# The last token block of a down projection in two column pieces, and part of each block's results through ScalarE and GpSimd

## The chip, the cores and the metric

The kernel runs on one core of one Trainium2 chip. The metric is the device time of one execution in microseconds (us), as the median of several runs. In this text PE is TensorE (PEld its weight load), DVE VectorE, ACT ScalarE, POOL GpSimd and SP the engine that issues most of the DMAs. L1197 is line 1197 of the kernel before; lines of the changed kernel are called new lines.

## The reference

One layer of a hybrid encoder for two request groups, 256 prompt rows and 128 sample rows, 384 rows of 2048 channels in all, in fp32: a mixer (pooling branch, state-space branch, gates, output projection) and an MLP, each between two RMS norms. The part that matters here is the end of the MLP:

```python
def rmsnorm(x, g):
    xf = x.astype(jnp.float32)
    y = xf * lax.rsqrt(jnp.mean(xf * xf, axis=-1, keepdims=True) + EPS)
    return (y * g.astype(jnp.float32)).astype(x.dtype)
...
    x = x + rmsnorm(m, p['g_mix_post'])
    hdn = jnp.square(jax.nn.relu(rmsnorm(x, p['g_mlp_pre']) @ p['w_up'])) @ p['w_down']
    x = x + rmsnorm(hdn, p['g_mlp_post'])
```

`w_up` is 2048 x 8192 and `w_down` 8192 x 2048. The last norm needs the sum of squares over all 2048 columns of a row before any element of that row can be finished.

## The kernel before

All matrix products keep fp32's precision by splitting each operand into a high part and a rest, both of type fp32r (a shortened fp32), and adding three matmuls: high x high, high x rest, rest x high. A weight unit of 128 x 1024 values is fetched by `wfetch` (L59, on SP's queue) and split by `wsplit` (L64): ACT copies it to fp32r (L68), DVE subtracts (L69).

The MLP runs in eight rounds, `c8`. A round makes eight slices of the hidden layer (line 1164 on; products in `proj`, relu and square on DVE and ACT) and then multiplies them by `w_down` in four column tiles `nb` of 512 columns. For this `moving` (L110) is called with three PSUM tiles `o[b]`, one for each block of 128 token rows. The activations are the stationary operand, loaded afresh for every matmul, and the weights are the moving one, 512 columns wide. Inside `moving`, `mm` (L114) issues the three matmuls of one depth of 128 rows (L118, L119, L120). A down tile has four weight units of two such depths each, so a block takes 4 x 2 x 3 = 24 matmuls.

In all tiles but the last, a unit is used for all three blocks and then dropped. In the last tile of the last round (`c8` = 7, `nb` = 3) `tail` is 4: all four units are kept, and the loop at L138 runs all 24 matmuls of block 0, then of block 1, then of block 2, calling `done(b)` after each, so that the closing work of one block runs under the matmuls of the next. The fourth unit has its own buffers `eh` and `el` (L133 to L136), since the pool has three.

`done` (L1177) closes a block of a down tile:

- DVE adds the PSUM tile to the accumulator `hacc` (L1182).
- In the last round ACT squares the result, with the row sums going to one column of `st3` for each tile (L1186).
- In tiles 0 to 2 DVE multiplies by the norm's gain `gpo` in place (L1188). In tile 3 DVE writes the product to its own tile `z3` (L1193).
- In tile 3 `postnorm` (L943) follows, on 128 x 1 operands: DVE sums the first three partial sums (L945 to L947, which can run early), ACT takes a root with the fourth (L948), DVE makes the fourth's own sum (L949), a reciprocal (L950) and a correcting step (L951, L953). The result is `y`, one factor for each row.
- For each of the four column tiles DVE computes `z * y + x1` (L1197, 512 columns; `x1` is the residual held in SBUF) and SP stores 256 KB (L1200).

A framework orders the work: each engine runs its instructions in the order in which it was given them (a scheduler may let ready work pass; `behind` ties an instruction to follow another), and waits on semaphores are set where one engine reads what another wrote, or writes what another still reads. SP issues its stores in order, each behind its own wait. POOL has had its last instruction, the load of `gpo` (L1156), long before; ACT issues no DMA in this kernel.

Of the kernel before, what the change touches and what calls it, by code (L numbers as in the profile page):

```python
# [14 lines left out]
P = 128  # L15
# [4 lines left out]
DM = 2048  # L20
# [13 lines left out]
def build(ctx, tc, io):  # L34
# [21 lines left out]
    def behind(ins):  # L56
        return nullcontext() if ins is None else tc.issue_after(ins.ins)
# [22 lines left out]
    last = [None]  # L80
# [26 lines left out]
            half(o, q, take(src, f"{name}_{q}"), rhs)  # L107
        return o

    def moving(o, units, lhs, tail, done, pool=None, own=0, hook=None):  # L110
        nk = 2 * len(units)
        n = len(units)

        def mm(b, wh, wl, k, k2):  # L114
            t = slice(b * P, b * P + P)
            c = slice(k2 * 512, k2 * 512 + 512)
            mh, ml = lhs[k][0][:, t], lhs[k][1][:, t]
            te.matmul(o[b], mh, wh[:, c], start=k == 0, stop=False)  # L118
            te.matmul(o[b], mh, wl[:, c], start=False, stop=False)  # L119
            last[0] = te.matmul(o[b], ml, wh[:, c], start=False, stop=k == nk - 1)  # L120

        for kp in range(n - tail):
            wh, wl = take(*units[kp])
            with behind(last[0] if chain[0] else None):
                for k2 in range(2):
                    for b in range(3):
                        mm(b, wh, wl, kp * 2 + k2, k2)
            if hook and kp in hook:
                hook[kp]()
        w = [wload(*units[kp]) for kp in range(n - tail, n - own)]  # L130
        for kp in range(n - own, n):
            f, name = wfetch(*units[kp])
            h = pool.tile([P, 1024], F32R, name=f"eh_{name}")  # L133
            l = pool.tile([P, 1024], F32R, name=f"el_{name}")
            s.activation(h, f, AF.Copy)
            v.tensor_tensor(l, f, h.bitcast(F32), ALU.subtract)  # L136
            w.append((h, l))
        for b in range(3):  # L138
            for i, (wh, wl) in enumerate(w):
                for k2 in range(2):  # L140
                    mm(b, wh, wl, (n - tail + i) * 2 + k2, k2)
            done(b)

    def three(name):
        return [sstile(f"{name}_{b}") for b in range(3)]
# [167 lines left out]
    with tc.tile_pool(name="phc", bufs=1, reuse_waits="tile") as pc, tc.tile_pool(name="phc2", bufs=2, reuse_waits="tile") as pc2:  # L313
# [75 lines left out]
        def gate_a(nb):  # L389
            o = three(f"pj_ga{nb}")  # L390
            sg = pc2.tile([P, 3, 512], F32, tag="sg", name=f"sg{nb}", bufs=1)

            def done(b):
                s.activation(sg[:, b], o[b], AF.Sigmoid, scale=yx[:, b : b + 1])

            moving(o, [(io["w_ga"][nb, kp], f"ga{nb}_{kp}") for kp in range(8)], xg, 0, done)
            return sg

        def pool_out(nb, sg):
            o = three(f"pj_pp{nb}")  # L400

            def done(b):
# [92 lines left out]
    def gate_b(nb, pool, tag, hook=None):  # L495
        o = three(f"pj_gb{nb}")
        n = NB * 256 if tag == "hs" else 1536
        t = pool.tile([P, n], F32, tag=tag, name=f"gbt{nb}")[:, :1536].rearrange("p (b n) -> p b n", b=3)

        def done(b):  # L500
# [400 lines left out]
    with ExitStack() as phe:  # L901
        pe1 = phe.enter_context(tc.tile_pool(name="phe", bufs=1, reuse_waits="tile"))
        pe2 = phe.enter_context(tc.tile_pool(name="phe2", bufs=3, reuse_waits="tile"))
        pe4 = phe.enter_context(tc.tile_pool(name="phe4", bufs=1, reuse_waits="tile"))
        ab = []

        def aload():
            for i in (len(ab), len(ab) + 1):
                a = pe2.tile([P, T], F32, tag="ar", name=f"ar{i}")
                sy.dma_start(a, a_scr[i])  # L910
                h = pe1.tile([P, T], F32R, name=f"abh{i}")
                l = pe1.tile([P, T], F32R, name=f"abl{i}")
                s.activation(h, a, AF.Copy)
                v.tensor_tensor(l, a, h.bitcast(F32), ALU.subtract)
                ab.append((h, l))

        for nb in (2, 3):
            gate_b(nb, pe4, "gbt", {kp: aload for kp in range(8)})
        chain[0] = False
        main.close()  # L920
        mp = mpool.enter_context(tc.tile_pool(name="mp", bufs=1, side="right", reuse_waits="tile"))
        for nb in range(4):
            ma = mp.tile([P, 3, 512], F32, tag="mar", name=f"mar{nb}", bufs=1)
            gb = pe4.tile([P, 1536], F32, tag="gbt", name=f"gbr{nb}").rearrange("p (b n) -> p b n", b=3)
            sy.dma_start(ma, ma_scr[nb])
            sy.dma_start(gb, gb_scr[nb])
            o = three(f"pj_sp{nb}")

            def done(b):
# [8 lines left out]
    x1 = res.tile([P, 3, DM], F32, name="x1")  # L938
# [1 line left out]

    root = [None]

    def postnorm(pool, st, b, name, doubled=False):  # L943
        pre, ms, rt, y = (pool.tile([P, 1], F32, tag=f"n{i}", name=f"n{i}_{name}{b}", bufs=3) for i in range(4))
        v.tensor_tensor(pre, st[:, b, 0:1], st[:, b, 1:2], ALU.add)  # L945
        v.tensor_tensor(pre, pre, st[:, b, 2:3], ALU.add)
        v.tensor_scalar(pre, pre, 1.0 / DM, EPS, ALU.mult, ALU.add)  # L947
        root[0] = s.activation(rt, st[:, b, 3:4], AF.Sqrt, bias=pre, scale=1.0 / DM)  # L948
        v.tensor_scalar(ms, st[:, b, 3:4], 1.0 / DM, pre, ALU.mult, ALU.add)  # L949
        v.reciprocal(y, rt)  # L950
# [11 lines left out]
    with tc.tile_pool(name="phf", bufs=1, side="right", reuse_waits="tile") as pf, tc.tile_pool(  # L962
# [19 lines left out]
        for nb in range(4):  # L982
# [5 lines left out]
            def done(b):  # L988
# [162 lines left out]
    with tc.tile_pool(name="phg", bufs=1, reuse_waits="tile") as pg, tc.tile_pool(  # L1151
# [7 lines left out]
        pg.tile([P, 112], F32, name="pad_e")  # L1159
        NC = 8  # L1160
        for c8 in range(NC):
            hh = []
# [11 lines left out]
            for nb in range(4):  # L1174
                o = [sstile(f"wd{c8}_{nb}_{b}") for b in range(3)]

                def done(b):  # L1177
                    dst = hacc[:, b, blk(nb)]
                    if c8 == 0:
                        s.copy(dst, o[b])  # L1180
                        return
                    v.tensor_tensor(dst, o[b], dst, ALU.add)  # L1182
                    if c8 < NC - 1:
                        return
                    q = pg2.tile([P, 512], F32, tag="q3", name=f"q3_{nb}_{b}")
                    s.activation(q, dst, AF.Square, accum_out=st3[:, b, nb : nb + 1])  # L1186
                    if nb < 3:
                        v.tensor_tensor(dst, dst, gpo[:, blk(nb)], ALU.mult)  # L1188
# [3 lines left out]
                    z3 = pg.tile([P, 512], F32, name=f"z3_{b}")  # L1192
                    v.tensor_tensor(z3, dst, gpo[:, blk(nb)], ALU.mult)  # L1193
                    y = postnorm(pg2, st3, b, "n3", doubled=True)
                    for i in range(4):
                        z = z3 if i == 3 else hacc[:, b, blk(i)]
                        v.scalar_tensor_tensor(  # L1197
                            out=z, in0=z, scalar=y, in1=x1[:, b, blk(i)], op0=ALU.mult, op1=ALU.add
                        )
                        sy.dma_start(io["y"][b][:, blk(i)], z)  # L1200

                moving(
                    o,
# [128 lines left out]
```

## Time and profile before

| | |
|---|---|
| median of 3 runs | 2812.53 us (2811.7 to 2814.31) |
| the profiled execution, its own time | 2813.31 us |
| its span, from the first to the last instruction | 2811.5 us |
| mean granted TensorE clock | 0.999 |
| HBM read, written | 407.11 MB, 41.72 MB |
| all DMA, mean | 161 GB/s |
| matmuls of the down projection, L118 | 296.3 us busy in x762, mean 389 ns |
| PSUM adds of the down projection, L1182 | 57.3 us busy in x84, mean 691 ns |
| stores of the last block, L1200 | 12 of 256 KB in all three blocks, 2.3 us from issue to landing |

A row of the profile names the line, the engine, the operation, the tile written and the tiles read, the shape and the count. A matmul's busy time includes the time to run through the array, so neighbours overlap: matmuls of 389 ns each start 0.227 us apart. What one costs in a row of many is the distance between two starts. In a timeline row the first number is the start in us from the beginning of the span and the second the duration; what stands in brackets is the engine's idle time before it and who ended it. The profile's spans on POOL are rough.

### The profile page before, as it was taken

To read this page: it belongs to the slowest core of one execution; us is meant where nothing else is said; L and a number is where in the kernel's file an instruction comes from. 1 tells how busy PE (TensorE), PEld (TensorE's weight loads), DVE (VectorE), ACT (ScalarE), POOL (GpSimd) and SP (SyncE) were. 2 spreads that over 40 slices of the span, in tenths; PEclk is the share of its full clock that TensorE was granted. 3 is DMA by queue.
4 is the path that set the end of the run, shared out by engine and by line. 5 is a ranking of instruction groups with operands and counts; after the bars stand their busy time and mean duration, and the time that the engine had idled before them with its cause. 6 is when DMAs were issued, how large, how long until landed. Compare 5 with 4: busy or idle time off the path is not lost.

```text
span 2811.5 us, 39083 instructions
## 1 busy us (share of the span) xinstructions
PE 2795.5 (99%) x15663; PEld 2545.3 (91%) x15663; DVE 1487.7 (53%) x1979; ACT 1167.9 (42%) x1830; POOL 119.5 (4%) x143
## 2 busy tenths in 40 slices
PE   9999999999999999999999999999999999999998
PEld 8998889999999999988888888989899998989897
DVE  6575335677777778756333336434444444444446
ACT  5443225456565646544322235433233332323233
POOL 0000000001110111010000000000000000000000
PEclk9999999999999999999999999999999999999999
DMA  7434445555565556557544543433333343333333
GB/s 268 132 125 150 139 139 199 180 187 207 198 225 191 201 198 223 195 185 232 177 145 162 180 144 115 140 128 128 128 128 128 128 128 128 128 129 128 131 127 122
DMA packets 140934, 451.39 MB, mean 161 GB/s; under 512 B 17808, under 2 KB 39632, under 8 KB 135760
## 3 DMA queue, kind: packets, MB, share of 16 engines
q1 hardware_dynamic: 132624, 412.97, 44.6%
q0 software_dynamic: 8128, 35.93, 3.3%
q8 instruction: 123, 2.02, 0.3%
q14 instruction: 59, 0.48, 0.1%
HBM read 407.11 MB, written 41.72 MB: 160 GB/s over the span
## 4 chain that ended last, share of the span: by engine, by line
PE 97%; ACT 1%; DVE 1%; DMA 0%; issue 0%; SPq 0%; DVEq 0%; ACTq 0%
PE pj_up L77 6%; PE pj_up L78 6%; PE pj_up L76 6%; PE wd L119 6%; PE wd L120 6%; PE wd L118 6%; PE pj_x L76 4%; PE pj_x L77 4%; PE pj_x L78 4%; PE pj_z L77 3%; PE pj_z L78 3%; PE pj_z L76 3%; PE pj_sp L119 3%; PE pj_sp L120 3%; PE pj_sp L118 3%; PE pj_ga L118 2%
## 5 line engine op out<-in xcount | busy, mean ns | idle before, releaser
L76 PE MATMUL pj_up<-x1h,wh_up 128*128 128x384 f32 x1024 | 342.6, 335 | 0.5 <-ACT x1h L1058 0.5
L78 PE MATMUL pj_up<-x1h,wl_up 128*128 128x384 f32 x1024 | 342.3, 334 | 0.7 <-DVE wl_up L69 0.7
L77 PE MATMUL pj_up<-x1l,wh_up 128*128 128x384 f32 x1024 | 342.3, 334 | 0.6 <-DVE x1l L1063 0.6
L120 PE MATMUL wd<-wh_wd,hl 128*128 128x512 f32 x762 | 296.6, 389 | 0.0
L119 PE MATMUL wd<-wl_wd,hh 128*128 128x512 f32 x762 | 296.6, 389 | 0.0
L118 PE MATMUL wd<-wh_wd,hh 128*128 128x512 f32 x762 | 296.3, 389 | 0.0
L69 DVE TENSOR_TENSOR wl_wd<-w_wd,wh_wd 128x1024 fp32r<-128x1024 f32 x127 | 155.6, 1226 | 261.9 <-ACT wh_wd L68 261.9
L68 ACT ACTIVATE wh_wd<-w_wd 128x1024 fp32r<-128x1024 f32 x127 | 134.8, 1061 | 350.8 <-PE wd L120 284.2
L68 ACT ACTIVATE wh_up<-w_up 128x1024 fp32r<-128x1024 f32 x128 | 135.9, 1062 | 323.8 <-PE pj_up L77 259.7
L69 DVE TENSOR_TENSOR wl_up<-w_up,wh_up 128x1024 fp32r<-128x1024 f32 x128 | 156.9, 1226 | 198.6 <-ACT wh_up L68 198.5
L76 PE MATMUL pj_x<-xgh,wh_x 128*128 128x384 f32 x768 | 258.2, 336 | 0.0
L78 PE MATMUL pj_x<-xgh,wl_x 128*128 128x384 f32 x768 | 256.6, 334 | 0.0
L77 PE MATMUL pj_x<-xgl,wh_x 128*128 128x384 f32 x768 | 256.6, 334 | 0.0
L77 PEld LDWEIGHTS pj_up<-x1l,wh_up 128*128 128x128 f32 x1024 | 192.2, 188 | 1.4 <-DVE x1l L1063 1.2
L76 PEld LDWEIGHTS pj_up<-x1h,wh_up 128*128 128x128 f32 x1024 | 192.2, 188 | 1.3 <-ACT x1h L1058 1.0
L78 PEld LDWEIGHTS pj_up<-x1h,wl_up 128*128 128x128 f32 x1024 | 192.2, 188 | 1.0 <-DVE wl_up L69 1.0
L78 PE MATMUL pj_z<-xgh,wl_z 128*128 128x384 f32 x512 | 171.0, 334 | 0.0
L76 PE MATMUL pj_z<-xgh,wh_z 128*128 128x384 f32 x512 | 171.0, 334 | 0.0
L77 PE MATMUL pj_z<-xgl,wh_z 128*128 128x384 f32 x512 | 171.0, 334 | 0.0
L120 PEld LDWEIGHTS wd<-wh_wd,hl 128*128 128x128 f32 x762 | 143.1, 188 | 29.7
L119 PEld LDWEIGHTS wd<-wl_wd,hh 128*128 128x128 f32 x762 | 143.1, 188 | 29.6 <-DVE wl_wd L69 0.2
L118 PEld LDWEIGHTS wd<-wh_wd,hh 128*128 128x128 f32 x762 | 143.1, 188 | 29.5
(318 smaller groups left out, 5789.8 us busy)
## 6 DMA issues: line engine op xcount, KB each, us to landing
w_up<-w_up SPq DMA_DIRECT2D x128, 512.0 KB, 3.4
w_wd<-w_down SPq DMA_DIRECT2D x128, 512.0 KB, 3.4
w_x<-w_in SPq DMA_DIRECT2D x96, 512.0 KB, 3.7
w_z<-w_in SPq DMA_DIRECT2D x64, 512.0 KB, 3.8
w_sp<-w_ssd SPq DMA_DIRECT2D x64, 512.0 KB, 3.4
w_ga<-w_ga SPq DMA_DIRECT2D x32, 512.0 KB, 3.5
w_pp<-w_pp SPq DMA_DIRECT2D x32, 512.0 KB, 3.5
hs<-ssm SPq DMA_DIRECT2D x16, 1024.0 KB, 5.6
```

What stands on the lines that cost most here:

```text
L68: s.activation(h, w, AF.Copy)
L69: v.tensor_tensor(l, w, h.bitcast(F32), ALU.subtract)
L76: te.matmul(out, wh, xh, start=first, stop=False)
L77: te.matmul(out, wh, xl, start=False, stop=False)
L78: return te.matmul(out, wl, xh, start=False, stop=last)
L118: te.matmul(o[b], mh, wh[:, c], start=k == 0, stop=False)
L119: te.matmul(o[b], mh, wl[:, c], start=False, stop=False)
L120: last[0] = te.matmul(o[b], ml, wh[:, c], start=False, stop=k == nk - 1)
```

## The change

Three things change, all in the last down tile of the last round.

The 512 columns of block 2 are made in two pieces, columns 0 to 383 and then 384 to 511, each with its own 24 matmuls and its own `done`; both pieces lie in the same PSUM tile. Only the first matmul of the first piece has the start flag. The order of the units is tied with `behind`. The sum of squares of the second piece goes to a fifth column of `st3`, and `postnorm` adds one more partial sum (`extra`).

In each of the three blocks the fourth column tile is finished in two parts: DVE does the first 128 columns as before, and the other 384 are multiplied by `y` on ACT (in place, new L1211) and have the residual added on POOL (new L1212).

The 384 columns are stored by a DMA of their own. In blocks 0 and 1 SP issues it after the block's other stores (new L1223). In block 2 ACT issues it (new L1214). The first 128 columns are stored by SP (new L1221).

```diff
-    def moving(o, units, lhs, tail, done, pool=None, own=0, hook=None):
+    def moving(o, units, lhs, tail, done, pool=None, own=0, hook=None, cut=None):
-        def mm(b, wh, wl, k, k2):
+        def mm(b, wh, wl, k, k2, c0=0, c1=512):
             t = slice(b * P, b * P + P)
-            c = slice(k2 * 512, k2 * 512 + 512)
+            c = slice(k2 * 512 + c0, k2 * 512 + c1)
+            ob = o[b][:, c0:c1]
...
+            te.matmul(ob, mh, wh[:, c], start=k == 0 and c0 == 0, stop=False, **how)
...
         for b in range(3):
-            for i, (wh, wl) in enumerate(w):
-                for k2 in range(2):
-                    mm(b, wh, wl, (n - tail + i) * 2 + k2, k2)
-            done(b)
+            for cc in (cut if b == 2 and cut else ((0, 512),)):
+                for i, (wh, wl) in enumerate(w):
+                    with behind(last[0] if cut else None):
+                        for k2 in range(2):
+                            mm(b, wh, wl, (n - tail + i) * 2 + k2, k2, *cc)
+                done(b, *cc)
...
-    def postnorm(pool, st, b, name, doubled=False):
+    def postnorm(pool, st, b, name, doubled=False, extra=False):
...
+        if extra:
+            v.tensor_tensor(pre, pre, st[:, b, 3:4], ALU.add)
+        end = st[:, b, 4:5] if extra else st[:, b, 3:4]
...
-        st3 = pg.tile([P, 3, 4], F32, name="st3")
+        st3 = pg.tile([P, 3, 5], F32, name="st3")
...
-                    v.tensor_tensor(dst, o[b], dst, ALU.add)
+                    v.tensor_tensor(dst, o[b][:, c0:c1], dst, ALU.add)
...
+                    n = nb + (c0 > 0)
+                    q = pg2.tile([P, 512], F32, tag="q3", name=f"q3_{n}_{b}")[:, : c1 - c0]
+                    s.activation(q, dst, AF.Square, accum_out=st3[:, b, n : n + 1])
...
+                    if c1 < 512:
+                        return
+                    v.tensor_tensor(z, hacc[:, b, blk(nb)], gpo[:, blk(nb)], ALU.mult)
+                    y = postnorm(pg2, st3, b, "n3", doubled=True, extra=c0 > 0)
+                    side = slice(P, 512)
+                    xb = x1[:, b, blk(3)]
+                    s.activation(z[:, side], z[:, side], AF.Copy, scale=y)
+                    gp.tensor_tensor(z[:, side], z[:, side], xb[:, side], ALU.add)
+                    if b == 2:
+                        s.dma_start(io["y"][b][:, 1536 + P :], z[:, side])
                     for i in range(4):
...
+                        if i == 3:
+                            d, e, yo = d[:, :P], e[:, :P], yo[:, :P]
+                        v.scalar_tensor_tensor(out=d, in0=d, scalar=y, in1=e, op0=ALU.mult, op1=ALU.add)
+                        sy.dma_start(yo, d)
+                    if b < 2:
+                        sy.dma_start(io["y"][b][:, 1536 + P :], z[:, side])
...
+                    cut=((0, 384), (384, 512)) if c8 == NC - 1 and nb == 3 else None,
```

The other callers of `moving` pass no `cut`, and their `done` takes the column bounds and ignores them.

More of the change, by code (lines that the diff above doesn't have):

```diff
@@ L391, in gate_a, with done @@
             sg = pc2.tile([P, 3, 512], F32, tag="sg", name=f"sg{nb}", bufs=1)
-            def done(b):
+            def done(b, *cc):
                 s.activation(sg[:, b], o[b], AF.Sigmoid, scale=yx[:, b : b + 1])
@@ L400, in pool_out, with done @@
             o = three(f"pj_pp{nb}")
-            def done(b):
+            def done(b, *cc):
                 v.tensor_tensor(sg[:, b], o[b], sg[:, b], ALU.mult)
@@ L498, in gate_b, with done @@
         t = pool.tile([P, n], F32, tag=tag, name=f"gbt{nb}")[:, :1536].rearrange("p (b n) -> p b n", b=3)
-        def done(b):
+        def done(b, *cc):
             s.activation(t[:, b], o[b], AF.Sigmoid, scale=yx[:, b : b + 1])
@@ L927, in build, with done @@
             o = three(f"pj_sp{nb}")
-            def done(b):
+            def done(b, *cc):
                 v.tensor_tensor(gb[:, b], o[b], gb[:, b], ALU.mult)
@@ L946, in postnorm @@
         v.tensor_tensor(pre, pre, st[:, b, 2:3], ALU.add)
+        if extra:
+            v.tensor_tensor(pre, pre, st[:, b, 3:4], ALU.add)
+        end = st[:, b, 4:5] if extra else st[:, b, 3:4]
         v.tensor_scalar(pre, pre, 1.0 / DM, EPS, ALU.mult, ALU.add)
-        root[0] = s.activation(rt, st[:, b, 3:4], AF.Sqrt, bias=pre, scale=1.0 / DM)
-        v.tensor_scalar(ms, st[:, b, 3:4], 1.0 / DM, pre, ALU.mult, ALU.add)
+        root[0] = s.activation(rt, end, AF.Sqrt, bias=pre, scale=1.0 / DM)
+        v.tensor_scalar(ms, end, 1.0 / DM, pre, ALU.mult, ALU.add)
         v.reciprocal(y, rt)
@@ L986, in build, with done @@
             o = [sstile(f"wo{nb}_{b}") for b in range(3)]
-            def done(b):
+            def done(b, *cc):
                 q = pf2.tile([P, 512], F32, tag="q", name=f"q1_{nb}_{b}", bufs=1)
@@ L1157, in build @@
         s.activation(gpo, gpo, AF.Copy, scale=-0.5)
-        st3 = pg.tile([P, 3, 4], F32, name="st3")
+        st3 = pg.tile([P, 3, 5], F32, name="st3")
         pg.tile([P, 112], F32, name="pad_e")
+        z3 = []
         NC = 8
@@ L1175, in build, with done @@
                 o = [sstile(f"wd{c8}_{nb}_{b}") for b in range(3)]
-                def done(b):
-                    dst = hacc[:, b, blk(nb)]
+                def done(b, c0, c1):
+                    dst = hacc[:, b, blk(nb)][:, c0:c1]
                     if c8 == 0:
@@ L1191, in done @@
                         pg.tile([P, 128], F32, name="pad_z")
-                    z3 = pg.tile([P, 512], F32, name=f"z3_{b}")
-                    v.tensor_tensor(z3, dst, gpo[:, blk(nb)], ALU.mult)
-                    y = postnorm(pg2, st3, b, "n3", doubled=True)
-                    for i in range(4):
[L1196 to L1200, printed above, removed]
+                    if c0 == 0:
+                        z3.append(pg.tile([P, 512], F32, name=f"z3_{b}"))
+                    z = z3[b]
+                    if c1 < 512:
[8 more added lines that the diff above has]
+                        s.dma_start(io["y"][b][:, 1536 + P :], z[:, side])
+                    for i in range(4):
+                        d, e = (z, xb) if i == 3 else (hacc[:, b, blk(i)], x1[:, b, blk(i)])
+                        yo = io["y"][b][:, blk(i)]
+                        if i == 3:
[4 more added lines that the diff above has]
+                        sy.dma_start(io["y"][b][:, 1536 + P :], z[:, side])
                 moving(
```

11 lines of the change are left out of this document (5 added, 6 removed).

## The prediction

> **What bounds the kernel now.** I read the page first, for which engine fills the span.
>
> ```profile
> span 2811.5 us, 39083 instructions
> PE 2795.5 (99%) x15663; PEld 2545.3 (91%) x15663; DVE 1487.7 (53%) x1979; ACT 1167.9 (42%) x1830; POOL 119.5 (4%) x143
> PE 97%; ACT 1%; DVE 1%; DMA 0%; issue 0%; SPq 0%; DVEq 0%; ACTq 0%
> ```
>
> TensorE works in 99% of the span and is 97% of the chain that ended last. Comparing the built programs engine by engine, with line numbers stripped, I found that the change leaves every instruction ahead of the last down tile as it was. So only the last 20 us can move, and I read those in the timeline (start, duration, engine, line).
>
> ```profile
> 2796.40 0.39 PE L118 MATMUL wd<-wh_wd,hh 128*128 128x512 f32 x1
> 2796.63 0.39 PE L119 MATMUL wd<-wl_wd,hh 128*128 128x512 f32 x1
> ...
> 2799.12 2.08 DVE L1197 SCALAR_TENSOR_TENSOR hacc<-hacc,n_n,x 128x512 f32<-128x512 f32 x3
> 2801.12 0.74 DVE L1197 SCALAR_TENSOR_TENSOR z<-z,n_n,x 128x512 f32<-128x512 f32 x1
> ...
> 2801.61 0.39 PE L120 MATMUL wd<-eh_wd,hl 128*128 128x512 f32 x1
> 2802.04 0.69 DVE L1182 TENSOR_TENSOR hacc<-wd,hacc 128x512 f32<-128x512 f32 x1 [0.18 <-PE wd L120]
> 2802.77 0.69 DVE L1193 TENSOR_TENSOR z<-hacc,gpo 128x512 f32<-128x512 f32 x1
> 2802.77 0.63 ACT L1186 ACTIVATE q<-hacc 128x512 f32<-128x512 f32 x1 [4.38 <-DVE hacc L1182]
> 2803.30 0.19 ACT L1186 ACTIVATION_READ_ACCUMULATOR q<-hacc 128x1 f32 x1
> 2803.52 0.21 DVE L949 TENSOR_SCALAR n_n<-st,n_n 128x1 f32<-128x1 f32 x1
> 2803.52 0.29 ACT L948 ACTIVATE n_n<-st,n_n 128x1 f32<-128x1 f32 x1
> 2803.85 0.16 DVE L950 RECIPROCAL n_n<-n_n 128x1 f32<-128x1 f32 x1
> ...
> 2804.55 2.08 DVE L1197 SCALAR_TENSOR_TENSOR hacc<-hacc,n_n,x 128x512 f32<-128x512 f32 x3
> 2806.54 0.75 DVE L1197 SCALAR_TENSOR_TENSOR z<-z,n_n,x 128x512 f32<-128x512 f32 x1
> 2807.41 0.33 SPq L1200 DMA_DIRECT2D y<-z  x1
> ```
>
> Token block 2's 24 matmuls run from 2796.40 to 2802.00 (2801.61 + 0.39). Then it is a chain with nothing beside it: add out of PSUM, square and read, root, reciprocal, y, from which the four last operations (two quoted rows) start at 2804.55; they end at 2807.29 and the last store is issued at 2807.41. Call the start of those four Y. In block 1 the same four run from 2799.12 to 2801.86 (2801.12 + 0.74), under block 2's matmuls. The first two DVE rows, block 1's last four, matter below: DVE is at work until just before block 2's matmuls end.
>
> **The change part by part.** *First piece of block 2.* 24 matmuls of 384 columns instead of 512. The nearest rows are the projections:
>
> ```profile
> 599.77 0.33 PE L76 MATMUL pj_z<-xgh,wh_z 128*128 128x384 f32 x1
> ...
> 603.93 0.33 PE L76 MATMUL pj_z<-xgh,wh_z 128*128 128x384 f32 x1
> ```
>
> 24 intervals in 4.16 us are 0.173 us each; the 512-column rows at 2796.40 and 2796.63 are about 0.227 apart. The piece therefore ends at 2796.40 + 23 x 0.173 + 0.33 = 2800.7.
>
> *A wait between the pieces.* In the built program the first 128-column matmul carries a wait on DVE, and the count it waits for is the one that DVE's 384-column add out of the same PSUM tile (new L1190) raises. All 23 matmuls behind it stand queued, and for them wait the second add, the norm and all stores of block 2. The add can't start at 2800.7: DVE then still works through block 1's last four. They start at 2799.12; the last of them has 128 columns now.
>
> ```profile
> L1137 DVE SCALAR_TENSOR_TENSOR dgl<-cst,n_n,dgh 128x128 fp32r<-128x128 f32 x3 | 1.0, 347 | 0.0
> L526 DVE TENSOR_TENSOR cbuf<-pj_x,rstd 128x384 f32<-128x384 f32 x48 | 26.6, 554 | 34.0 <-PE pj_x L78 33.9
> L334 DVE TENSOR_TENSOR pbuf<-pj_p,rstd 128x128 f32<-128x128 f32 x16 | 4.5, 279 | 0.0
> ```
>
> 2801.12 + 0.35 = 2801.47, less 0.07 that neighbours overlap (2799.12 + 2.08 = 2801.20 against the next start, 2801.12): the add starts at 2801.40, takes 0.55, and PE goes on at about 2801.98. That is when all of block 2 was through before; TensorE has stood for 1.3 us. Without the cover of block 1's work it would be 0.7 us earlier, 2801.3.
>
> [...]
>
> *Second piece.* 24 matmuls of 128 columns of fp32r, each with its own weights. No row has this; bounds from rows:
>
> ```profile
> L118 PEld LDWEIGHTS wd<-wh_wd,hh 128*128 128x128 f32 x762 | 143.1, 188 | 29.5
> L613 PEld LDWEIGHTS Y<-E,xdt 128*32 128x32 f32 x768 | 21.3, 110 | 8.2 <-issue 2.7
> ...
> 485.49 1.04 PE L574 MATMUL cb<-xs,xs 128*128 128x256 f32 x6
> 486.36 0.49 PE L568 MATMUL trB<-cst,xs 128*128 128x128 f32 x3
> L568 PE MATMUL trB<-cst,xs 128*128 128x128 f32 x24 | 3.9, 273 | 0.0
> ```
>
> Below: 512 against 384 columns differ by 0.053 us, so by columns alone it is 0.173 - 2 x 0.053 = 0.067. Middle: the weight load. 96 columns more cost 188 - 110 = 78 ns, so 128 columns occupy the loader for about 0.104; and the three trB matmuls of 128 columns, each with a load, stand (0.49 - 0.273) / 2 = 0.109 apart. Above: plain fp32 (cb) runs each product in two records; 512 columns took 486.36 - 485.49 = 0.87 us, 0.217 per 128. I take 0.109, since fp32r runs one record at 384 and 512 columns and nothing hides the load at 128: 23 x 0.109 + 0.27 = 2.78, end at 2804.76. Against 2802.00 that is **+2.76** (by the bounds +1.7 and +5.3).
>
> [...]
>
> *After the last matmul.* The add has 128 columns: 0.28 for 0.69, -0.41. The square of the first piece and the third partial sum's add run under the second piece; the last square has 128 columns (some 0.3 us less of the 0.73 from 2802.77 to 2803.49), but the multiply by gpo is still 512 wide on DVE (0.69), and DVE's next step queues behind it. So the reciprocal comes about 0.9 after the add instead of 1.11 (2803.85 - 2802.74): -0.2. Together **-0.6**, and Y = 2804.55 + 2.76 - 0.6 = 2806.7.
>
> *The last four and the side path.* DVE now ends at Y + 2.34 (2.0 + 0.35) instead of Y + 2.74. But 384 columns go through ACT (0.61 by the first row below) and then POOL.
>
> ```profile
> L241 ACT ACTIVATE xgh<-x,x0g 128x384 fp32r<-128x384 f32 x15 | 8.6, 607 | 5.4 <-DMA x<-xT 5.4
> L772 POOL TENSOR_TENSOR ssum<-ssum,ysq x24: 1014/1178/5315, 539.6 to 1244.6; 128x384 f32<-128x384 f32 x24
> ...
> 634.97 2.28 DVE L718 TENSOR_TENSOR hs<-hs,decb 128x2048 f32<-128x2048 f32 x1
> 639.45 0.55 DVE L526 TENSOR_TENSOR cbuf<-pj_x,rstd 128x384 f32<-128x384 f32 x1
> ...
> 635.09 5.32 POOL L772 TENSOR_TENSOR ssum<-ssum,ysq 128x384 f32<-128x384 f32 x1 [0.78 <-ACT ysq L771]
> ```
>
> The same add on POOL takes 1.01 at best and 5.3 at worst. In the worst case it began while DVE ran operations with two SBUF inputs back to back from 634.97, and it ended 0.96 after DVE's first operation with a PSUM input started (639.45). The four operations at Y have two SBUF inputs each, back to back, so I let POOL's add finish 1.0 after them: Y + 3.35, ACT's issue at Y + 3.45. Before, the last issue was at Y + 2.86 (2807.41): **+0.6**. If POOL isn't held, it is done by Y + 1.7, and the last issue is SP's at Y + 2.46, -0.4 at best.
>
> ```profile
> y<-z SPq DMA_DIRECT2D x3, 256.0 KB, 2.3
> ...
> 2804.90:2808.30 3.40, 0.00 (x0) 0.00 (x0) 2.39 (x4) 0.00 (x0) 0.00 (x0) 0.50 0.63 235
> ```
>
> The first row says that a store lands 2.3 us after its issue; I leave that, and the 1.8 us from 2809.7 to the span's end, as they are. (The second row is a stretch of the span: its length, busy time of PE, its weight load, DVE, ACT and POOL, granted clock, DMA share and GB/s.) ACT's queue issues no store before; its issue is put at SP's 0.33. In blocks 0 and 1 SP's queue holds the side store, waiting for POOL, ahead of the next block's stores. By the same reckoning POOL is done with block 1 at 2801.4 + 1.0 = 2802.4, long before Y, so that wait costs nothing; behind ACT's store in block 2 stands nothing.
>
> The sum is +2.76 - 0.6 + 0.6 = **+2.8 us**. The profiled execution took 2813.31 for its span of 2811.5; the median of the runs shown is 2812.53. I forecast **2815.3** on the median (2816.1 on the profiled execution), 0.1% more.
>
> **The rivals.** *Four cycles a column*: fp32r falls to fp32's pace at 128 columns. For it: the cb rows; against: one record per fp32r product. It decides at an interval over 0.2 us; 2.5 more, +5.3, 2817.8, slower than before by about the bound. *The clock falls*: TensorE stands for 1.3 us between the pieces; the row just quoted shows the granted clock at 0.50 once PE had stopped for 2.9 us. Against: the gap is shorter. Decided by a granted clock of 0.5 from 2802 on, the second piece costs 0.218 each, +5.3 or more (2818). *The pieces stream as one*: the count that PE waits for is reached in time, and loads are hidden. 24 x (0.173 + 0.067) = 5.76 against 24 x 0.227 = 5.44, and a last matmul shorter by 0.16: +0.2, 2812.7, not slower. Against: the count is the add's. Decided by a gap under 0.2 us. *POOL isn't held*: -1.0 from the sum, +1.8, 2814.3; that the side path gains nothing at the end then follows too.
>
> **How the numbers follow.** Forecast 0.52, four cycles 0.30, clock 0.05, one stream 0.05, POOL free 0.08. The range 2812.9 to 2818.8 takes in the bounds +1.7 and +5.3 and a median's spread of about 1 us; the forecast's own is 2814.3 to 2816.3. A measurement of this kernel can tell about 0.2%, 5.6 us, from no change. Over it: half of four cycles (0.15), the clock (0.05), a twelfth of the forecast for terms that I have too small: 0.25. Under it on the fast side: 0.02. Within: 0.73.
>
> **What would show it.** The first 128-column matmul starts at about 2802.0, right behind DVE's 384-column add, which starts when block 1's last operation ends; the 128-column matmuls stand 0.109 apart and end at 2804.8; block 2's POOL add ends 1 us after DVE's last operation and is the last thing ahead of a store. The forecast is wrong if PE's gap is under 0.5 us, if the interval is near 0.07 or 0.22, or if SP's store of 128 columns is issued after ACT's.

## The result, and the profile after

The changed kernel takes 2817.57 us (median of 21 runs, 2815.48 to 2819.04) against 2813.09 for the kernel before (21 runs, 2811.66 to 2815.73): a ratio of 1.0015, 95% interval 1.0009 to 1.0021. It is slower by 4.5 us on the median, where 2.8 were forecast. Its profiled execution took 2815.95 us for a span of 2814.2, near the lower end of its runs.

This is the timeline of the changed kernel's last 20 us (start, duration, engine, new line; in brackets the idle time before it and who ended it):

```profile
2795.79 0.33 PE L120 MATMUL wd<-wh_wd,hh 128*128 128x384 f32 x1
...
2798.65 2.81 DVE L1220 SCALAR_TENSOR_TENSOR hacc<-hacc,n_n,x 128x512 f32<-128x512 f32 x3
2799.35 1.56 POOL L1212 TENSOR_TENSOR z<-z,x 128x384 f32<-128x384 f32 x1 [3.93 <-ACT z L1211]
...
2799.81 0.34 PE L122 MATMUL wd<-eh_wd,hl 128*128 128x384 f32 x1
...
2801.65 0.55 DVE L1190 TENSOR_TENSOR hacc<-wd,hacc 128x384 f32<-128x384 f32 x1
...
2802.25 0.33 PE L120 MATMUL wd<-wh_wd,hh 128*128 128x128 f32 x1 [2.10 <-DVE hacc L1190]
...
2804.31 0.28 PE L120 MATMUL wd<-eh_wd,hh 128*128 128x128 f32 x1
2804.43 0.33 PE L121 MATMUL wd<-el_wd,hh 128*128 128x128 f32 x1
2804.55 0.42 PE L122 MATMUL wd<-eh_wd,hl 128*128 128x128 f32 x1
2804.76 0.41 PE L120 MATMUL wd<-eh_wd,hh 128*128 128x128 f32 x1
...
2805.19 0.41 PE L122 MATMUL wd<-eh_wd,hl 128*128 128x128 f32 x1
...
2807.43 2.89 DVE L1220 SCALAR_TENSOR_TENSOR hacc<-hacc,n_n,x 128x512 f32<-128x512 f32 x3
2808.12 0.99 POOL L1212 TENSOR_TENSOR z<-z,x 128x384 f32<-128x384 f32 x1 [7.21 <-ACT z L1211]
...
2809.15 0.37 ACTq L1214 DMA_DIRECT2D y<-z  x1
...
2810.78 0.41 SPq L1221 DMA_DIRECT2D y<-z  x1
```

Three things are to be seen. TensorE waits 2.10 us between the pieces for DVE's 384-column add, as forecast, but longer than the 1.28 forecast: POOL's add in block 1 (2799.35) runs between DVE's operations, and DVE's three take 2.81 us where they took 2.08 before. They also start 2.86 us after block 2's first matmul instead of 2.72, since POOL held DVE in block 0 as well (its three take 2.84 us there; without the side path, in the first run below, the start is at 2.70). The 128-column matmuls stand 0.111 us apart until 2804.43, and from 2804.55 on 0.21. And at the end it is not POOL that waits for DVE but DVE for POOL (three in 2.89), so SP's 64 KB store is the last, not ACT's.

Why the last matmuls are slow is in two stretches of the same span (length; busy time and count of PE, its weight load, DVE, ACT, POOL; granted clock; DMA share; GB/s):

```profile
2804.00:2804.40 0.40, 0.40 (x6) 0.40 (x5) 0.00 (x0) 0.00 (x0) 0.00 (x0) 1.00 0.00 0
2804.60:2805.60 1.00, 1.00 (x5) 0.82 (x4) 0.00 (x0) 0.00 (x0) 0.00 (x0) 0.50 0.00 0
```

TensorE's granted clock falls from 1.00 to 0.50 inside the second piece. Without that it would have ended 2.89 us after its start (as in the fourth, seventh and ninth runs below), at 2805.14 instead of 2805.60 (2805.19 + 0.41): 0.46 us.

Block 2's first matmul starts 0.61 us earlier than in the profile of before (2795.79, there 2796.40), though nothing was changed ahead of it: this is one execution against another. From that start on the two are compared, with Y the start of DVE's last operations as in the prediction:

| us | before | forecast | after |
|---|---|---|---|
| block 2 on TensorE, first start to last end | 5.60 | 8.36 | 9.81 |
| of it the gap between the pieces | 0 | 1.28 | 2.10 |
| of it the second piece | - | 2.78 | 3.35 |
| last matmul's end to Y | 2.55 | 1.95 | 1.83 |
| Y to the last store's issue | 2.86 | 3.45 | 3.35 |
| Y to the span's end | 6.95 | 7.55 | 6.77 |

From block 2's start the tail is 18.41 us long instead of 15.10, 3.3 more. The profiled execution shows only 2.7 more because its tail began 0.6 earlier.

### The profile page after: what moved, and what is told of

It reads as the page before. It is cut to its first block, busy times and chain, and to the rows that moved or that the text cites. A ratio compares the mean times of both kernels' runs of the same rounds, so it can differ in the third digit from the quotient of the medians.

```text
span 2814.2 us, 39150 instructions
## 1 busy us (share of the span) xinstructions
PE 2798.0 (99%) x15687; PEld 2548.2 (91%) x15687; DVE 1489.5 (53%) x1981; ACT 1170.5 (42%) x1835; POOL 123.7 (4%) x146
## 3 DMA queue, kind: packets, MB, share of 16 engines
q8 instruction: 123, 2.02, 0.3%
## 4 chain that ended last, share of the span: by engine, by line
PE 96%; DMA 2%; DVE 1%; ACT 1%; issue 0%; SPq 0%; DVEq 0%; ACTq 0%
PE pj_up L78 6%; PE pj_up L77 6%; PE pj_up L76 6%; PE wd L121 6%; PE wd L122 6%; PE wd L120 6%; PE pj_x L76 5%; PE pj_x L78 5%; PE pj_x L77 5%; PE pj_z L76 3%; PE pj_z L78 3%; PE pj_z L77 3%; PE pj_sp L121 3%; PE pj_sp L122 3%; PE pj_sp L120 3%; PE pj_ga L120 2%
## 5 line engine op out<-in xcount | busy, mean ns | idle before, releaser
L120 PE MATMUL wd<-wh_wd,hh 128*128 128x512 f32 (+1 forms) x768 | 297.8, 388 | 2.1 <-DVE hacc L1190 2.1
L121 PE MATMUL wd<-wl_wd,hh 128*128 128x512 f32 (+1 forms) x768 | 298.0, 388 | 0.0
L122 PE MATMUL wd<-wh_wd,hl 128*128 128x512 f32 (+1 forms) x768 | 297.9, 388 | 0.0
```

Source lines behind the costliest of these rows:

```text
L120: te.matmul(ob, mh, wh[:, c], start=k == 0 and c0 == 0, stop=False, **how)
L121: te.matmul(ob, mh, wl[:, c], start=False, stop=False, **how)
L122: last[0] = te.matmul(ob, ml, wh[:, c], start=False, stop=k == nk - 1, **how)
```

## The experiments

Lines in the rows below are each kernel's own; "before" ran beside each group of runs, with medians of 2813.16 to 2813.30.

### 1. The cut without the side path

```diff
-                    s.activation(z[:, side], z[:, side], AF.Copy, scale=y)
-                    gp.tensor_tensor(z[:, side], z[:, side], xb[:, side], ALU.add)
...
-                        if i == 3:
-                            d, e, yo = d[:, :P], e[:, :P], yo[:, :P]
...
```

> The cut into 384 and 128 columns stays; the side path is gone (DVE finishes all 512 columns of the last tile, SP stores 256 KB). Theory A (the loss is the wait between the pieces, the second piece's own pace and where the clock falls in it; the side path pays for itself): block 1's last four operations are no longer stretched by POOL, so TensorE stands about 1.6 to 1.8 us between the pieces instead of 2.1 (DVE's last operation of block 1 has 512 columns again, 0.4 more than forecast with 128); 128-column matmuls 0.11 apart at full clock, 0.21 after the clock has fallen; the last store's issue to the span's end 4.1 us as before the change; time about 2.4 us above before if the clock holds, up to 4.5 if it falls at the start of the piece. Rival B (the side path is what costs): within 1 us of before. Rival C (the pace of the second piece alone costs): TensorE's gap would not depend on what DVE does, 2.1 us again.

Measured: 2816.57 us, 3.4 above before (ratio 1.0013, 1.0004 to 1.0022). From its timeline:

```profile
2798.17 2.08 DVE L1211 SCALAR_TENSOR_TENSOR hacc<-hacc,n_n,x 128x512 f32<-128x512 f32 x3
...
2801.44 0.33 PE L120 MATMUL wd<-wh_wd,hh 128*128 128x128 f32 x1 [1.62 <-DVE hacc L1190]
...
2805.28 0.41 PE L122 MATMUL wd<-eh_wd,hl 128*128 128x128 f32 x1
```

DVE's three are back at 2.08 and the gap is 1.62, of which 0.4 is that DVE's fourth operation has 512 columns again (0.75 us for 0.34). From 2802.72 on the 128-column matmuls stand 0.21 apart instead of 0.11, as in the change where the granted clock is 0.50, so the second piece took 4.25 us (2801.44 to 2805.69), 1.36 more than 2.89. Most of the loss is there without the side path; rival B falls.

### 2. The side path without the cut

```diff
-                    cut=((0, 384), (384, 512)) if c8 == NC - 1 and nb == 3 else None,
+                    cut=((0, 512),) if c8 == NC - 1 and nb == 3 else None,
```

> No cut (24 matmuls of 512 columns in block 2); the side path through ACT and POOL with its stores stays. Theory A: block 2's matmuls keep 0.227 us apart and the clock stays up to their end; in the last block DVE is held about 0.5 us by POOL, and the last store has 64 KB and reaches the span's end 3.4 us after its issue instead of 4.1: together within 1 us of before (about -0.2). Rival B (the side path is what costs): +3 us or more with no change on TensorE.

Measured: 2813.51 us, 0.35 above before (1.0001, 0.9993 to 1.0010): no difference that can be told. In the timeline DVE's three operations of block 1 take 2.92 beside POOL, and block 2's add starts 0.36 after the last matmul's end (2799.93 + 0.39) instead of 0.04:

```profile
2797.57 2.92 DVE L1220 SCALAR_TENSOR_TENSOR hacc<-hacc,n_n,x 128x512 f32<-128x512 f32 x3
...
2799.93 0.39 PE L122 MATMUL wd<-eh_wd,hl 128*128 128x512 f32 x1
...
2800.68 0.68 DVE L1190 TENSOR_TENSOR hacc<-wd,hacc 128x512 f32<-128x512 f32 x1
```

So POOL's hold of DVE in block 1 has a price here too, 0.3 us; with the cut it lengthens TensorE's gap instead.

### 3. The second piece in a PSUM tile of its own

```diff
-            ob = o[b][:, c0:c1]
+            ob = o[3][:, : c1 - c0] if c0 else o[b][:, c0:c1]
...
-            te.matmul(ob, mh, wh[:, c], start=k == 0 and c0 == 0, stop=False, **how)
+            te.matmul(ob, mh, wh[:, c], start=k == 0, stop=False, **how)
...
```

> Both pieces as in the change, but the second piece accumulates in a PSUM tile of its own, so that no matmul waits for DVE's 384-column add; side path as in the change. Theory A: TensorE goes on within 0.1 us; 128-column matmuls 0.111 apart, the whole of block 2 about 24 x (0.173 + 0.111) = 6.8 us against 5.45 before, so +1.3 on TensorE, -0.5 behind it, -0.2 from the side path: about +0.6 against before, 3 to 4 us less than the change. DVE's first add now comes late (behind block 1's last four) but still before the second piece ends. Rival C (the second piece's pace is the loss): the 24 matmuls take 3.3 us or more again and the time stays within 1 us of the change. Rival D (the clock falls because the matmuls are narrow, not because TensorE stands): the granted clock falls to 0.5 before the last matmul here too.

Measured: 2813.54 us, 0.4 above before (1.0002, 0.9994 to 1.0011), 4 below the change. In its timeline the last matmul of the first piece, and the first and last of the second:

```profile
2799.60 0.33 PE L122 MATMUL wd<-eh_wd,hl 128*128 128x384 f32 x1
...
2799.77 0.22 PE L120 MATMUL wd<-wh_wd,hh 128*128 128x128 f32 x1
...
2802.29 0.28 PE L122 MATMUL wd<-eh_wd,hl 128*128 128x128 f32 x1
```

The matmuls run on without a gap, 0.11 apart, and the clock holds to their end. Block 2 takes 6.98 us (2795.59 to 2802.57), so the narrow pieces cost 1.4 on TensorE, and 0.6 of that comes back behind it. The wait, with what it does to the clock, was most of the loss; rivals C and D fall.

### 4. TensorE kept busy in the gap

```diff
+                if cc[1] == 384:
+                    idle = sstile("idle")
+                    with behind(last[0]):
+                        for _ in range(8):
+                            last[0] = te.matmul(idle, lhs[0][0][:, :P], w[0][0][:, :512], start=True, stop=True)
```

> The change with eight more 512-column matmuls into an unused PSUM tile between the two pieces (work that no output needs), which fill some 1.8 us of TensorE's gap; the wait for DVE's add stays behind them. Theory A: the second piece starts when it did (the wait is DVE's, not TensorE's), but the granted clock stays at 1.00 through it, all 24 matmuls stand 0.111 apart; the profile's tail is 0.6 us shorter than the change's, and the median is 1 to 1.5 us below the change's, since no run loses clock in the second piece. Rival D (the clock's fall has nothing to do with the gap): the last matmuls are 0.21 apart again and the median equals the change's. Rival E (the fall costs nothing on the median): clock up, median equal to the change's within 0.5 us.

Measured: 2816.36 us, 3.2 above before (1.0011, 1.0002 to 1.0020), 1.2 below the change's median. In the timeline the second piece's first matmul:

```profile
2803.35 0.33 PE L120 MATMUL wd<-wh_wd,hh 128*128 128x128 f32 x1 [0.36 <-DVE hacc L1195]
```

And the stretch that holds the piece, with the granted clock behind the busy times:

```profile
2803.40:2806.20 2.80, 2.80 (x24) 2.71 (x24) 0.31 (x2) 0.55 (x2) 0.00 (x0) 1.00 0.51 187
```

With the same wait but only 0.36 us of standing, the clock stays at 1.00 and the piece takes 2.90. The clock fell in the change because TensorE stood. The two medians come from different groups of runs and their intervals overlap, so the 1.2 agrees with the forecast without proving it; the granted clock does not depend on the median.

### 5. The change once more

> [...] Rival D (the fall is a fixed delay after TensorE stops): it falls 4.35 us after the first piece's end again.

Measured: 2816.68 us (11 runs; 1.0013, 1.0004 to 1.0021), with the change's first 21 runs a median of 2817.45 over 32, against 2813.22 over the 102 runs of before: 4.2 more. The second piece in its timeline:

```profile
2801.85 0.33 PE L120 MATMUL wd<-wh_wd,hh 128*128 128x128 f32 x1 [2.11 <-DVE hacc L1190]
...
2802.79 0.34 PE L122 MATMUL wd<-wh_wd,hl 128*128 128x128 f32 x1
2802.93 0.41 PE L120 MATMUL wd<-wh_wd,hh 128*128 128x128 f32 x1
...
2805.92 0.41 PE L122 MATMUL wd<-eh_wd,hl 128*128 128x128 f32 x1
```

The gap is the same, 2.11; but the pace goes from 0.11 to 0.21 1.0 us into the piece (2802.79 to 2802.93) instead of 2.25, and the piece takes 4.48 us (to 2806.33), 1.59 over 2.89. So the fall comes at another place with the same standing. Rival D (a fixed delay) falls: 4.35 us behind the first piece's end in the first profile, about 3.1 here. What sets the place is not shown.

### 6. and 7. Two edits that did something else

The sixth moved block 1's last four operations behind block 2's first add in the source (`late` holds block 1's side path, last four operations and stores); the seventh replaced them by plain adds.

```diff
                     if c1 < 512:
+                        late.pop()()
                         return
```

> The change with DVE's order altered: block 1's last four operations and their stores are issued behind block 2's first add out of PSUM (and its square), instead of ahead of it; nothing else. [...] Rival F (what waits is tied to the PSUM tile whatever DVE does): the gap stays at 2.1 us.

```diff
-                        v.scalar_tensor_tensor(out=d, in0=d, scalar=y, in1=e, op0=ALU.mult, op1=ALU.add)
+                        v.tensor_tensor(d, d, e, ALU.add)
```

> The change with the last four operations as a plain add of the residual (the multiplication by y is left out there, in columns 0 to 1663 of each row), so that DVE runs plain two-input adds back to back there instead of operations with a scalar operand. Theory A as the prediction had it (DVE's operations with two inputs in SBUF shut POOL out while they follow each other): POOL's add in blocks 1 and 2 begins but ends only after the last of DVE's four, 2.5 us or more long, as in line 772's worst case, and DVE's three take 2.08 or less. Rival G (POOL gets in between any two of DVE's operations): POOL takes 1.0 to 1.6 us and DVE's three 2.8, as in the change.

In the sixth the framework's scheduler put three of the four operations ahead of the add again, since they were ready, so it stayed open how much of the gap is DVE's queue and how much the PSUM tile: gap 2.02, clock fallen after 0.6 us of the piece, 2817.40 us. The seventh leaves out the multiplication by y, so its one time (2811.96 us) can't be compared. Its plain adds no longer need y, so they ran early, with no POOL beside them, and what POOL does beside plain adds stayed open. But it left DVE idle when the first piece ended, as its timeline shows:

```profile
2799.77 0.56 DVE L1190 TENSOR_TENSOR hacc<-wd,hacc 128x384 f32<-128x384 f32 x1 [1.71 <-PE wd L122]
...
2800.39 0.33 PE L120 MATMUL wd<-wh_wd,hh 128*128 128x128 f32 x1 [0.65 <-DVE hacc L1190]
```

With DVE free the tile costs 0.65 us, and the clock held through the second piece (0.11 between its matmuls to the end, 2.89 us in all). Both questions were put again in 9 and 10.

### 8. Two pieces of 256 columns without waits

```diff
-                    cut=((0, 384), (384, 512)) if c8 == NC - 1 and nb == 3 else None,
+                    cut=((0, 256), (256, 512)) if c8 == NC - 1 and nb == 3 else None,
...
+                        for c in (slice(0, 384), slice(384, 512)) if (b, i) == (2, 3) else (slice(0, 512),):
...
```

The second piece has a tile of its own, as in 3, and the side path is gone, as in 1.

> A version of the same idea without its waits: two pieces of 256 columns, the second in a PSUM tile of its own; no side path; block 2's last tile finished and stored in 384 and 128 columns by DVE and SP. Theory A: no gap on TensorE; 256-column matmuls 0.111 to 0.120 apart, block 2 takes 5.4 to 5.9 us against 5.45 (0 to +0.4); the add behind the last matmul 0.27 less and the square 0.2 less (about -0.4); three operations 2.08 and then 0.57 and 0.34, last issue at Y + 2.95 against Y + 2.86 (+0.1); last store 64 KB, 3.45 from issue to the end against 4.09 (-0.65). Sum -0.5 to -0.9 against before, too small for the median to tell surely; 4 to 5 us below the change. Rival C (narrow pieces cost whatever the waits): TensorE's block 2 takes 6.5 us or more and the time is above before.

Measured: 2813.42 us, 0.1 above before (1.0001, 0.9992 to 1.0010). Block 2 took 5.92 us without a gap, 0.12 between matmuls, and Y to the span's end was 6.7. The expected gain behind the last matmul is missing, and the timeline says why:

```profile
2803.68 0.75 DVE L1212 SCALAR_TENSOR_TENSOR z<-z,n_n,x 128x512 f32<-128x512 f32 x1
2804.34 0.42 DVE L1190 TENSOR_TENSOR hacc<-wd,hacc 128x256 f32<-128x256 f32 x1
2804.92 0.42 DVE L1190 TENSOR_TENSOR hacc<-wd,hacc 128x256 f32<-128x256 f32 x1 [0.16 <-PE wd L122]
```

The first piece's add stands behind block 1's operations until 2804.34, almost to the end of the second piece, so its square is late too, and Y comes only 2.40 after the last matmul, against 2.55 before. A cut gains what DVE has free by then, and here that is little.

### 9. Block 1's operations tied behind the add

```diff
-                    v.tensor_tensor(dst, o[b][:, c0:c1], dst, ALU.add)
+                    out = v.tensor_tensor(dst, o[b][:, c0:c1], dst, ALU.add)
...
                     if c1 < 512:
+                        with behind(out):
+                            late.pop()()
                         return
...
```

> As the sixth run was meant: block 1's last four operations are tied behind block 2's first add out of PSUM, so that DVE is free when the first piece ends. Theory A (the add's own 0.65 us is all that the PSUM tile costs, the other 1.4 of the gap is DVE's queue): gap 0.65 us; the granted clock stays at 1.00 through the second piece, so 128-column matmuls 0.111 apart and block 2 takes 4.36 + 0.65 + 2.89 = 7.9 us from first start to last end, against 5.6 before; block 1's four end about when the second piece does and may hold its add by some 0.3; against before +2.3 - 0.7 + 0.3 - 0.2 = +1.7, so a median near 2815, 1.5 to 2.7 below the change's. Rival F (the gap is tied to the PSUM tile): 2 us again. Rival D (narrow matmuls or any gap lower the clock): clock 0.5 in the second piece again, median within 1 us of the change's.

Measured: 2814.86 us, 1.6 above before (1.0005, 0.9996 to 1.0014), where +1.7 was expected, and 2.6 below the 32 runs of the change. Its timeline shows the add right behind the first piece, and the second piece:

```profile
2801.40 0.56 DVE L1191 TENSOR_TENSOR hacc<-wd,hacc 128x384 f32<-128x384 f32 x1 [1.57 <-PE wd L122]
...
2802.01 0.33 PE L120 MATMUL wd<-wh_wd,hh 128*128 128x128 f32 x1 [0.65 <-DVE hacc L1191]
...
2804.63 0.27 PE L122 MATMUL wd<-eh_wd,hl 128*128 128x128 f32 x1
```

The stretch of the second piece:

```profile
2802.10:2804.80 2.70, 2.70 (x24) 2.66 (x24) 2.32 (x6) 0.51 (x2) 0.00 (x0) 1.00 0.70 264
```

Gap 0.65, granted clock 1.00 to the end, second piece 2.89 us. Of the change's 2.10 us of standing 1.45 were DVE's queue, POOL's hold included, and only 0.65 the shared tile. That undoes the larger part of the loss with the same cut, the same tile and the same side path.

### 10. Plain adds beside POOL

```diff
-                        v.scalar_tensor_tensor(out=d, in0=d, scalar=y, in1=e, op0=ALU.mult, op1=ALU.add)
+                        with behind(factor[0]):
+                            v.tensor_tensor(d, d, e, ALU.add)
...
```

> As the seventh run was meant: the plain adds of the residual (the multiplication by y is left out there, in columns 0 to 1663 of each row) are tied behind the step that makes y, so that they run beside POOL's add. Theory A as the prediction had it (DVE's plain operations with two inputs in SBUF shut POOL out while they follow each other): POOL's add ends only behind the last of DVE's four in blocks 1 and 2, 2.0 us or more long instead of 1.0 to 1.6, and DVE's three take about 2.0. Rival G (POOL gets in between any two of DVE's operations): POOL takes 1.0 to 1.6 us and DVE's three 2.8, as in the change.

This kernel too leaves out the multiplication, and there is one execution (2815.60 us), so only its rows are read. Block 1 in its timeline:

```profile
2798.00 2.69 DVE L1222 TENSOR_TENSOR hacc<-hacc,x 128x512 f32<-128x512 f32 x3
...
2798.82 1.33 POOL L1213 TENSOR_TENSOR z<-z,x 128x384 f32<-128x384 f32 x1 [4.04 <-ACT z L1212]
```

POOL takes 1.33 and DVE's three 2.69: POOL gets in between two of DVE's operations of this size, with a scalar operand or without. Rival G holds, and what the prediction took from line 772's worst case did not carry over. What held POOL for 5.3 us there stays open.

### 11. The small last store alone

```diff
+                        for c in (slice(0, 384), slice(384, 512)) if (b, i) == (2, 3) else (slice(0, 512),):
...
-                        sy.dma_start(io["y"][b][:, blk(i)], z)
+                            q = s if c.start else sy
+                            q.dma_start(io["y"][b][:, blk(i)][:, c], z[:, c])
```

> The kernel before with one edit: block 2's last tile is finished in 384 and then 128 columns by DVE, the first stored by SP and the last, 64 KB, by ACT's queue. Theory A (what the side path won at the end is the size of the last store alone): TensorE as before; last issue at Y + 2.9 against Y + 2.86; from there to the span's end 3.4 to 3.5 us against 4.09: -0.5 to -0.6, a median of 2812.5 to 2813, within the measurement's noise of before. Rival H (the end is a fixed time behind the last issue): 4.1 us again and no gain.

Measured: 2813.16 us, 0.1 below before (1.0000, 0.9991 to 1.0009). The last issues are at Y + 2.86 and 2.90 (Y = 2804.30), but the span ends 7.1 after Y. Two stretches, the first of before, the second of this run:

```profile
2806.25:2809.00 2.75, 0.00 (x0) 0.00 (x0) 1.04 (x2) 0.00 (x0) 0.00 (x0) 0.50 0.99 371
```

```profile
2806.00:2808.75 2.75, 0.00 (x0) 0.00 (x0) 1.17 (x3) 0.00 (x0) 0.00 (x0) 0.50 1.00 368
```

For 2.75 us the DMA engines are busy at a share of 0.99 and 1.00. Block 2's output is 1 MB; at 371 GB/s that is 2.8 us. So in these two kernels the stores already fill the DMA engines, and how the last of them is cut or queued made no difference. Rival H is nearer, but the time behind the last issue is not fixed: 4.2 us here, 3.4 in the change. Those 3.4 us were no gain either: with (6.77) and without (6.78) the side path Y to the end is the same. In the change, though, the DMA engines are not busy throughout (a share of 0.36 from 2809.70 to 2810.20), so the bytes alone don't explain why its end comes out the same; that is not shown.

### What the runs come to

Segments of the profiles (us; 7 and 10 leave out the multiplication and are not listed) and what they sum to against before's 15.10, beside the difference of the medians:

| run | block 2 on TensorE | gap | to Y | Y to end | sum - 15.10 | medians |
|---|---|---|---|---|---|---|
| the change | 9.81 | 2.10 | 1.83 | 6.77 | +3.3 | +4.5 |
| 1 cut alone | 10.22 | 1.62 | 1.83 | 6.78 | +3.7 | +3.4 |
| 2 side path alone | 5.60 | 0 | 2.86 | 6.92 | +0.3 | +0.4 |
| 3 own PSUM tile | 6.98 | 0 | 2.16 | 6.77 | +0.8 | +0.4 |
| 4 gap filled | 9.46 | 0.36 | 1.83 | 6.72 | +2.9 | +3.2 |
| 5 the change again | 10.94 | 2.11 | 1.83 | 6.74 | +4.4 | +3.4 |
| 6 add not moved | 11.19 | 2.02 | 1.83 | 6.84 | +4.8 | +4.1 |
| 8 256 columns | 5.92 | 0 | 2.40 | 6.71 | -0.1 | +0.1 |
| 9 add first | 7.89 | 0.65 | 1.83 | 6.77 | +1.4 | +1.6 |
| 11 small last store | 5.61 | 0 | 2.54 | 7.10 | +0.2 | -0.1 |

No run here is surely faster than before; 2, 3, 8, 9 and 11 can't be told from it. In all five profiles of this cut in which TensorE stands 1.6 us or more (the change, 1, 5, 6 and 10) the clock falls inside the second piece (0.21 us between its last matmuls in the change, 1, 5 and 10), which takes 3.35 to 4.81 us; in the four in which it stands 0.65 us or less (3, 4, 7 and 9) it does not, and the piece takes 2.80 to 2.90.

## Why the forecast came out as it did

The forecast was 2815.3 (+2.8), and the median is 2817.57 (+4.5). That is inside the stated range, but outside the forecast's own 2814.3 to 2816.3, and nearer to what two rivals gave, 2817.8 and 2818. The first of them, fp32's pace at 128 columns (0.217 us in the cb rows, 1.70 ns a column; 128 more columns of fp32r cost 0.053 us, 0.41 ns a column), did not happen, with 0.111 at full clock; the second, the fall of the clock, did in part. One of the forecast's own signs of being wrong came too: SP's store of 128 columns is issued after ACT's (2810.78 and 2809.15). So the direction and the range were right, and three terms of the sum were not: the wait was put 0.8 us too short, the clock at nothing where it cost 1.3 on average, and the end 0.8 too dear. That the first and the last cancel is luck. That the profiled execution shows +2.7, as forecast, is chance as well: its start was 0.6 us early, and its clock fell late.

- **First piece: right.** 0.173 us a matmul; 4.30 forecast, 4.36 measured (2795.79 to 2800.15).
- **The wait between the pieces: the mechanism right, the term mis-sized.** The step said that the add "starts at 2801.40" behind block 1's last four and that TensorE stands 1.3 us. It took the duration of the three from the kernel before (2.08), though the change itself puts a POOL add beside them. They take 2.81, which is 0.73 more, and start 0.14 later behind block 2's first matmul; the first piece ends 0.06 later. That makes 1.28 + 0.73 + 0.14 - 0.06 = 2.09, and TensorE stands 2.10 and 2.11 us in the two profiles. Runs 1 and 9 split it: 0.65 for the shared tile, about 0.56 for DVE's queue without POOL (1.62 of run 1 less 0.65, and less 0.41 for its wider fourth operation), and about 0.9 for POOL's hold. Run 3 shows the wait on the tile gone when the second piece has a tile of its own (gap 0).
- **The second piece's pace: right at full clock.** 0.111 us for the 0.109 taken from the trB matmuls; the bounds 0.067 and 0.217 are not what these fp32r pairs show at full clock.
- **The clock: a rival with too small a chance.** It had 0.05, with "the gap is shorter" against it, by a row that showed the clock low 2.9 us after TensorE had stopped. That row can't bound it: it shows how late after TensorE's last matmul the clock was low, not how short a gap lowers it. In the change 2.10 us of standing was followed by the fall, 2.25 us after TensorE had gone on (granted clock 1.00 from 2804.30 to 2804.50, 0.51 from 2804.50 to 2804.70); in run 9 0.65 us was not, within the piece. Between 0.65 and 1.62 us of standing no run of this cut lies, so where the bound is, if there is one, is not shown. In the five profiles of this cut with a gap of 1.6 us or more the fall cost 0.46, 1.12, 1.36, 1.59 and 1.92 us (second piece less 2.89), 1.3 on average. The rival as written, low from 2802 on, is the worst case of it.
- **After the last matmul: right.** -0.6 forecast, -0.72 measured, the same in six runs.
- **The last four and the side path: right at the last issue for the wrong reason, and wrong at the end.** +0.6 was forecast because DVE would hold POOL; POOL held DVE, the last issue came 0.49 later and was SP's. The step that failed is the next one, "a store lands 2.3 us after its issue; I leave that": the end does not follow the last issue, which lies 3.4 us ahead of it in the change and 4.1 to 4.2 in before and run 11. In these last two the DMA engines are busy with block 2's 1 MB, and Y to the end is 6.7 to 7.1 in every run of the table, with the side path or without.

Put right, the sum is +0.06 (first piece), 2.10, 2.89 and 1.3 for the clock in place of 1.28 and 2.78: block 2 takes 4.36 + 2.10 + 2.89 + 1.3 = 10.65 us, 5.05 more than before; less 0.72 behind it and 0.2 at the end, +4.1. The 32 runs show +4.2. What the forecast lacked was 0.8 us of DVE's queue and 1.3 of clock; what it had too much was 0.8 at the end.

## What to carry to other kernels

If a matmul's columns are cut for overlap, put the pieces into PSUM tiles of their own (in run 3 the gap went from 2.10 to 0 with that, and even so it only came out even with before), and ask first what stands in the reading engine's queue when the first piece is ready: here two thirds of the stall was other work in DVE's queue, and putting the add ahead of it gave back most of the loss. When a change puts work on an engine beside another, price the other's operations anew (here 2.81 us for 2.08), at every place where both run and not only where the change is aimed. Before shortening the last store, look at the DMA share at the end: where it was 0.99 and 1.00, a smaller last store gained nothing.

## What the runs showed that was not expected

The clock's fall is not confined to the tail. In the fourth run's profile, far from any edit, TensorE waits for the norm ahead of the up projections (stretches as above):

```profile
1736.00:1739.00 3.00, 1.81 (x15) 1.33 (x13) 2.64 (x8) 1.83 (x7) 0.00 (x0) 1.00 0.02 5
1740.20:1743.20 3.00, 3.00 (x11) 3.00 (x10) 3.00 (x9) 2.50 (x8) 0.00 (x0) 0.50 0.00 0
```

After a stretch with 1.2 of 3 us standing the clock was 0.50 with TensorE busy all the time, and only 11 matmuls ran in 3 us. In the profiles of before and of the change, with the same program ahead of the tail, TensorE stands there for 1.52 us, in three gaps of 0.86, 0.46 and 0.20, and the granted clock is 1.00 in both stretches; in the change 17 matmuls run in the second. So the wait for the norm cost clock in one execution and not in two others; 1.52 us of standing left the clock up here, and 1.62 in the tail of run 1 did not. What decides it is not shown. The fall may be part of the spread of about 4 us between executions of one kernel; that was not tested.
